# MLA scores of a hybrid attention layer: 289 contracted rows as 128 + 128 + 33 instead of 97 + 96 + 96

## The chip, the cores and the metric

The kernel runs on one core of a Trainium2 chip (trn2). The metric is device time in microseconds (us), the median of three runs; lower is better. The engines of the core are TensorE (PE, its weight loads listed apart as PEld), VectorE (DVE), ScalarE (ACT), GpSimd (POOL) and SyncE (SP, which here issues DMAs).

## The reference, cut to what matters

One layer in float32. From one input projection it computes two token mixers over the same 2048 latent tokens and 256 context tokens, gates them, projects them and merges them. The mixer that the change touches is multi-head latent attention (MLA, 8 heads):

```python
qa = concatenate([qa_n, rope_2d(qa_r)], -1)        # 64 + 32 = 96 columns a head
ka = concatenate([ka_n, broadcast(rope_2d(kr))])   # 64 of the head, 32 shared by all heads
sc = einsum('bqhd,bkhd->bhqk', qblk, k) * 96 ** -0.5
p  = softmax(sc, axis=-1)                          # over 2048 latent and 256 context keys
o  = einsum('bhqk,bkhd->bqhd', p, v)
```

The other mixer is a neighbourhood attention over a 32 x 64 grid; its matmuls are woven into the same stretch of the kernel.

## The kernel before, in words

Float32 accuracy comes from splitting a factor into a high and a low part (type float32r) and adding three products: high x high, high x low, low x high. A first part of the kernel (projections, to about 1057 us) writes the split queries `qm` and keys `kmS`, `krS` to DRAM; a last part (from about 2185 us) does the output projections. The change lies in the attention between them.

That attention goes over `u` = 0 to 31, a head `h` and a block `g` of 512 queries each. For each `u` there are nine steps `kp` (L1262), and each step handles two key tiles `x` of 128 keys. For one key tile the score tile `S` (128 keys x 512 queries, one PSUM bank) is the sum of three matmuls (L1275): `Kh` (96 rows of the high keys and a row of ones) with `qh` (96 rows of the high queries and a row with minus the maximum of each query), 97 contracted rows; `Kh` with `ql` (low queries), 96; `Kl` (low keys) with `qh`, 96. ScalarE then writes `P` = exp(`S`) (L1278).

Around the scores the order of TensorE is the order of the program (L809 pins it). `more` (L1264) issues tasks of the next `u`: 20 matmuls `pm` with the keys, whose maxima VectorE takes (L824, L825), and a fold. In a step of the middle of a `u` two of them stand behind the first score tile and one at the end of the step. `row` (L831), in step 8, turns the maxima into the row of `qh` by a matmul `pmf` and a ScalarE copy (L834). `feed` (L1171) issues the items of the neighbourhood attention (`ns` scores, `nm` and `nc` maxima, `nf`), by a weight, twice a step: behind the first score tile (L1283) and at the end (L1304). `pv` (L1229) multiplies `P` with the values; it collects two steps, so that steps 2, 4, 6 and 8 hold a burst of eight matmuls `oacc`, step 0 one of four, and steps 1, 3, 5 and 7 none. `oacc` is in float32 with 64 columns of weights, the even key tile in one half of the array's columns and the odd one in the other. `zp` and `nz` use quarters of 32 columns. `held` keeps the neighbourhood's own products `no` (also 64 columns) for the end of a burst (L1296).

All of `S`, `pm`, `pmf`, `zp`, `ns`, `nm`, `nc`, `nf` take their PSUM bank from one rotation of five (`psm`, L140): three turns in a pool of three banks and two in a pool of two; a tile waits until the last reader of the bank that it gets is done. GpSimd adds up `P` for the denominators (`za`, L1288) and spreads the maxima (L812). Queries are loaded by `load_qh` and `load_ql` (L773, L779), keys by `load_k` and `load_rope` (L785, L795), on SP's queue; the first of them are issued early, in the first part of the kernel. `P` has 8 buffers (`PB`), the spread maxima `nmd` of the neighbourhood two (L904).

Of the kernel before, what the change touches and what calls it, by code (L numbers as in the profile page):

```python
# [19 lines left out]
P = 128  # L20
# [7 lines left out]
NOPE = 64  # L28
# [26 lines left out]
STAT0 = 300  # L55
NQ = 8
HELD = 2
PB = 8
ZDVE = {1: tuple(range(1, 9))}
NPB = 6  # L60
BIG = -float(2 ** 100)
# [3 lines left out]
def tile_hybrid_layer(ctx: ExitStack, tc: tile.TileContext, I: dict, out: bass.AP, dbg=None):  # L65
# [43 lines left out]
    def bc(ap):  # L109
        return ap.bitcast(F32)  # L110
# [656 lines left out]
    KA = na.tile([P, NK], F32R, name="KA")  # L767
    KBt = na.tile([113, NK], F32R, name="KBt")
    QQ = na.tile([P, S], F32R, name="QQ")
    Kh = [(mk0, mk)[i].tile([DK + 1, NK], F32R, name=f"Kh{i}") for i in range(2)]  # L770
    Kl = [(mk0, mk)[i].tile([DK, NK], F32R, name=f"Kl{i}") for i in range(2)]

    def load_qh(u):  # L773
        h, g = divmod(u, NB)
        qh = mq.tile([DK + 1, W], F32R, tag="qh", name=f"qh{u}", bufs=3)
        env["q"].dma_start(bc(qh[0:DK, :]), bc(qm[h][0, :, g * W:(g + 1) * W]))
        return qh

    def load_ql(u):  # L779
        h, g = divmod(u, NB)  # L780
        ql = mq.tile([DK, W], F32R, tag="ql", name=f"ql{u}")
        env["q"].dma_start(bc(ql), bc(qm[h][1, :, g * W:(g + 1) * W]))
        return ql

    def load_k(h):  # L785
        i = h % 2
        env["q"].dma_start(bc(Kh[i][0:NOPE, :]), bc(kmS[h][0]))
        env["q"].dma_start(bc(Kl[i][0:NOPE, :]), bc(kmS[h][1]))

    def load_v(h):  # L790
        vt = mv.tile([P, NKT, DV], F32, tag="V", name=f"V{h}")
# [1 line left out]
        return vt  # L793

    def load_rope(i):  # L795
        env["q"].dma_start(bc(Kh[i][NOPE:DK, :]), bc(krS[:, 0, :]))
        env["q"].dma_start(bc(Kl[i][NOPE:DK, :]), bc(krS[:, 1, :]))
        nc.gpsimd.memset(bc(Kh[i][DK:DK + 1, :]), 1.0)

    zdefer = []  # L800
    onesr = mz.tile([P, P], F32R, name="onesr", bufs=1)
# [4 lines left out]
    def mm(*args, **kw):  # L806
        ins = nc.tensor.matmul(*args, **kw)  # L807
        if pe["pin"]:
            tc.keep_in_program_order(ins)  # L809
# [2 lines left out]
        nc.gpsimd.tensor_tensor(dst, ident.unsqueeze(1).to_broadcast([P, 4, P]), col.unsqueeze(2).to_broadcast([P, 4, P]),  # L812
                                op=ALU.mult)

    def max_tasks(u, qh):
        i = (u // NB) % 2
        m5 = mq.tile([P, 4, 5], F32, tag="m5", name=f"m5{u}")
        m1 = mq.tile([P, 4], F32, tag="m1", name=f"m1{u}")
        md = mq.tile([P, 4, P], F32R, tag="md", name=f"md{u}", bufs=1)

        def part(qt, ci):
            a, b = ci * W, min(NK, (ci + 1) * W)
            pm = psm(f"pm{u}_{qt}_{ci}")
            mm(pm[:, :b - a], qh[0:DK, qt * P:(qt + 1) * P], Kh[i][0:DK, a:b], start=True, stop=True)  # L824
            nc.vector.reduce_max(m5[:, qt, ci:ci + 1], pm[:, :b - a], axis=AX.X)  # L825

        def fold():
            nc.vector.tensor_reduce(m1, m5, axis=AX.X, op=ALU.max, negate=True)
            spread(md, m1)

        def row():  # L831
            pm = psm(f"pmf{u}")
            mm(pm, onesr, md.rearrange("p t f -> p (t f)"), start=True, stop=True)
            nc.scalar.activation(qh[DK:DK + 1, :], pm[DK:DK + 1, :], AF.Copy)  # L834
            for f in zdefer:
                f()
            zdefer.clear()

        return [lambda q=qt, c=ci: part(q, c) for qt in range(4) for ci in range(5)] + [fold], row
# [31 lines left out]
    def n_max(h, bn):  # L871
        mx = nv.tile([P, 2, 16], F32, tag="nmx", name=f"nmx{h}")
        m1 = nv.tile([P, 16], F32, tag="nm1", name=f"nm1{h}")
        kg = grid(NKm[:, 0:S])
        neg = -3.0e38

        def win(qb):
            rb, cb = divmod(qb, 4)
            (r0, r1), (c0, c1) = NROW[rb], CREG[cb]
            nr, ncl = r1 - r0, c1 - c0  # L880
            pm = psm(f"nm{h}_{qb}")
            pv_ = pm[:, :nr * ncl].rearrange("p (r c) -> p r c", c=ncl)
            mm(pv_, NQs[:, qb * P:(qb + 1) * P], kg[:, r0:r1, c0:c1], start=True, stop=True)
            rr, cc_ = r0 - rb * 8 + 4, c0 - cb * 16 + 8
            jk = npl.tile([P, W], F32, tag="njk", name=f"njk{h}_{qb}", bufs=1)
            nc.vector.tensor_tensor_reduce(
                out=jk[:, :nr * ncl].rearrange("p (r c) -> p r c", c=ncl), in0=pv_,
                in1=bn[:, rr:rr + nr, cc_:cc_ + ncl], scale=1.0, scalar=neg,
                op0=ALU.add, op1=ALU.max, accum_out=mx[:, 0, qb:qb + 1])

        def cmax(b2):
            pm = psm(f"nc{h}_{b2}")
            for x in range(2):
                qb = 2 * b2 + x
                mm(pm[:, x * C:(x + 1) * C], NQs[:, qb * P:(qb + 1) * P], NKm[:, S:NK],
                                 start=True, stop=True)
            nc.vector.reduce_max(mx[:, 1, 2 * b2:2 * b2 + 2], pm.rearrange("p (x c) -> p x c", x=2), axis=AX.X)

        mds = [None] * 4

        def turn(rb):
            if rb == 0:
                nc.vector.tensor_reduce(m1, mx.rearrange("p t q -> p q t"), axis=AX.X, op=ALU.max, negate=True)
            mds[rb] = npl.tile([P, 4, P], F32R, tag="nmd", name=f"nmd{h}_{rb}")  # L904
            spread(mds[rb], m1[:, rb * 4:rb * 4 + 4])

        def fin(rb):
            pm = psm(f"nf{h}_{rb}")
            mm(pm, onesr, mds[rb].rearrange("p t f -> p (t f)"), start=True, stop=True)
            nc.vector.tensor_copy(rowcol(QLt[64:65, rb * W:(rb + 1) * W]), blk(pm[64:65, :]))  # L910

        o = []
        for b2 in range(8):
            o += [lambda q=2 * b2: win(q), lambda q=2 * b2 + 1: win(q), lambda b=b2: cmax(b)]

        def last(k):
            if k < 4:
                turn(k)
            if k > 0:
                fin(k - 1)  # L920

        return o + [lambda k=k: last(k) for k in range(5)]

# [219 lines left out]

    with tc.high_priority(offset=HOIST):
        env["q"] = nc.sync
        qhs = [load_qh(0)]
        load_rope(0)
        load_k(0)
        qls = [load_ql(0)]
        qhs.append(load_qh(1))  # L1150
        env["q"] = nc.sync
    nc.sync.dma_start(bc(NKm[64:NM, :]), bc(cS[0][0:48, :]))
    nc.sync.dma_start(bc(NQs[64:NM, :]), bc(cS[1][0:48, 0:S]))
# [6 lines left out]
    load_rope(1)  # L1160
    env["q"] = nc.sync
    with tc.high_priority(offset=HOIST):
        tasks, row = max_tasks(0, qhs[0])
        for f in tasks + [row]:
            f()

# [79 lines left out]
    for u in range(nu):  # L1246
        h, g = divmod(u, NB)
        i = h % 2
        qh, ql = qhs[u], qls[u]
        vt = Vt  # L1250
        tasks, row = [], None
        if u + 2 < nu:
            qhs.append(load_qh(u + 2))
        if u + 1 < nu:
            tasks, row = max_tasks(u + 1, qhs[u + 1])
        if g == NB - 1 and h + 1 < H:
            Vt = load_v(h + 1)
        acc = psO.tile([P, W], F32, tag="O", name=f"oacc{u}")
# [3 lines left out]
        for kp in range(NKP):  # L1262
            pt = mp.tile([P, 2, W], F32, tag="P", name=f"P{u}_{kp}", bufs=PB)
            def more(frac):  # L1264
                nonlocal done
                want = min(len(tasks), int(len(tasks) * (kp + frac) / (NKP - 2.0) + 1))
                while done < want:
                    tasks[done]()
                    done += 1

            for x in range(2):
                ks = slice((2 * kp + x) * P, (2 * kp + x + 1) * P)
                sp = psm(f"S{u}_{kp}_{x}")
                n = 0
                for a, b, e in ((Kh[i], qh, DK + 1), (Kh[i], ql, DK), (Kl[i], qh, DK)):  # L1275
                    mm(sp, a[0:e, ks], b[0:e, :], start=(n == 0), stop=(n == 2))
                    n += 1
                nc.scalar.activation(pt[:, x, :], sp, AF.Exp)  # L1278
                more(0.33 * x)
                if x == 0 and kp == NKP - 1 and row is not None:  # L1280
                    row()
                if x == 0:
                    feed(total_weight * (step + 0.5 - LEAD) / (nsteps - TAIL - LEAD))  # L1283
            ve = nc.vector if kp in ZDVE.get(nu - u, ()) else nc.gpsimd
            if kp == 1:
                ve.tensor_tensor(za, prev, pt, op=ALU.add)
            elif 1 < kp < NKP - (u + 1 == nu):
                ve.tensor_tensor(za, za, pt, op=ALU.add)  # L1288
            prev = pt
            if kp == 1 and u + 1 < nu:  # L1290
                qls.append(load_ql(u + 1))
            if g == 0 and kp == 1 and h + 1 < H:
                load_k(h + 1)
            if pend is not None:
                ftasks = pv(*pend) or ftasks
                if env.pop("burst", False):  # L1296
                    while held:
# [246 lines left out]
```

## Time and profile before

| what | value |
|---|---|
| median of 3 runs | 2565.34 us (2562.31 to 2571.34) |
| the profiled execution: time | 2569.03 us |
| the profiled execution: span | 2567.2 us |
| mean granted TensorE clock | 0.987 |
| PE busy, all of the span | 2505.7 us (98%) |
| PE busy, 1057 to 2185 us | 1097.56 of 1128 us |

A busy time is a union of instructions of an engine, and a matmul's own duration contains the way through the array, so that durations of neighbours overlap. What a matmul costs in a stream is read from the distance of two starts. `128*64` in a row is the part of the array that is used, rows by columns. A releaser behind `<-` is what ended an engine's idle time.

### The profile page before, as it was taken

The numbers are of one execution on the slowest core, as the hardware profiler recorded it, in microseconds if no ns is written. First come the engines' busy times: TensorE is split into PE (matmuls) and PEld (weight loads), VectorE is DVE, ScalarE is ACT, GpSimd is POOL, SyncE is SP. The second block draws the span as 40 slices with busy tenths as digits, with TensorE's granted clock in tenths as the row PEclk, the third lists the DMA queues.
The fourth block names the chain that finished last, engine by engine and source line by source line (L and its number), as shares of the span: only waits on it lengthen the run. The fifth ranks groups of instructions, "written<-read, shape, count | busy, mean of one in ns | idle before, by whom it ended". The sixth has DMA issues, their size and how long they took to land.

```text
span 2567.2 us, 34839 instructions
## 1 busy us (share of the span) xinstructions
PE 2505.7 (98%) x12796; PEld 1839.1 (72%) x12796; DVE 1102.7 (43%) x2285; ACT 905.3 (35%) x1774; POOL 1092.2 (43%) x861
## 2 busy tenths in 40 slices
PE   7999999999999999999999999999999999999998
PEld 4878888877789888656555656665656664888998
DVE  4653222222311211355455635554646446455654
ACT  3664432222222122234444434444444444212221
POOL 1312111111310000368787868777887885132220
PEclk9999999999999999999999989999999999999999
DMA  7535765456553465712324141514140334765542
GB/s 263 191 92 164 257 222 185 140 167 191 178 159 109 122 214 194 184 48 68 80 51 107 46 101 36 121 39 109 39 110 26 81 106 144 246 190 161 181 148 70
DMA packets 182979, 342.86 MB, mean 134 GB/s; under 512 B 25130, under 2 KB 95950, under 8 KB 175438
## 3 DMA queue, kind: packets, MB, share of 16 engines
q1 hardware_dynamic: 168872, 299.01, 38.9%
q0 software_dynamic: 13504, 41.35, 5.6%
q8 instruction: 100, 1.64, 0.3%
q14 instruction: 71, 0.58, 0.1%
q10 hardware_dynamic: 432, 0.28, 0.0%
HBM read 214.42 MB, written 126.13 MB: 133 GB/s over the span
## 4 chain that ended last, share of the span: by engine, by line
PE 88%; DVE 3%; DMA 3%; POOL 2%; issue 2%; ACT 1%; SPq 1%; POOLq 0%; ACTq 0%; DVEq 0%
PE accm L135 25%; PE S L807 15%; PE oacc L807 10%; PE pm L807 6%; PE f L135 5%; PE ya L135 4%; PE vacc L135 4%; PE nacc L226 3%; PE no L807 3%; PE accf L135 2%; PE accx L135 1%; PE qa_False L135 1%; PE pstl L185 1%; PE nm L807 1%; POOL za L1288 1%
## 5 line engine op out<-in xcount | busy, mean ns | idle before, releaser
L825 DVE TENSOR_REDUCE m<-pm 128x1 f32<-128x512 f32 (+1 forms) x640 | 387.6, 632 | 420.0 <-PE pm L807 414.3
L1288 POOL TENSOR_TENSOR za<-za,P 128x1024 f32<-128x1024 f32 x217 | 516.1, 2378 | 114.2 <-ACT P L1278 110.7
L1278 ACT ACTIVATE P<-S 128x512 f32<-128x512 f32 x576 | 342.9, 597 | 481.3 <-PE S L807 465.9
L135 PE MATMUL accm<-hh,whi 128*128 128x512 f32 x928 | 366.7, 395 | 0.0
L135 PE MATMUL accm<-hh,wlo 128*128 128x512 f32 x928 | 366.4, 395 | 0.0
L135 PE MATMUL accm<-hl,whi 128*128 128x512 f32 x928 | 366.3, 395 | 0.0
L807 PE MATMUL oacc<-P,V 128*64 128x512 f32 x1152 | 292.0, 624 | 0.0
L807 PE MATMUL S<-qh,Kh 97*128 97x512 f32 x576 | 240.4, 417 | 7.9 <-DVE m L825 4.3
L807 PE MATMUL S<-ql,Kh 96*128 96x512 f32 x576 | 230.7, 400 | 0.0
L807 PE MATMUL S<-qh,Kl 96*128 96x512 f32 x576 | 229.3, 398 | 0.0
L807 PE MATMUL pm<-Kh,qh 96*128 96x512 f32 (+1 forms) x640 | 222.6, 395 | 4.5 <-DVE m L825 3.3
L135 PEld LDWEIGHTS accm<-hh,whi 128*128 128x128 f32 x928 | 174.1, 188 | 42.8 <-issue 0.8
L135 PEld LDWEIGHTS accm<-hh,wlo 128*128 128x128 f32 x928 | 174.1, 188 | 42.5
L135 PEld LDWEIGHTS accm<-hl,whi 128*128 128x128 f32 x928 | 174.1, 188 | 41.6
L807 PEld LDWEIGHTS pm<-Kh,qh 96*128 96x128 f32 x640 | 121.1, 189 | 106.7 <-issue 62.5
L135 PE MATMUL ya<-u,woh 128*128 128x256 f32 x1024 | 185.0, 283 | 2.0 <-DVE t L1346 2.0
L807 PEld LDWEIGHTS oacc<-P,V 128*64 128x64 f32 x1152 | 70.4, 139 | 137.6 <-issue 137.3
L135 PE MATMUL f<-wfh,y 128*128 128x512 f32 (+1 forms) x528 | 162.2, 387 | 6.2 <-DMA wfh<-wfS 4.0
L135 PEld LDWEIGHTS ya<-u,woh 128*128 128x128 f32 x1024 | 160.1, 192 | 3.2 <-DVE t L1346 2.4
L807 PEld LDWEIGHTS S<-qh,Kh 97*128 97x128 f32 x576 | 109.9, 191 | 54.0 <-issue 12.4
L135 PE MATMUL ya<-u,wol 128*128 128x256 f32 x512 | 144.8, 283 | 0.0
L356 ACT ACTIVATE g<-accm 128x512 f32<-128x512 f32 x88 | 52.2, 593 | 248.8 <-PE accm L135 202.6
(1928 smaller groups left out, 4253.2 us busy)
## 6 DMA issues: line engine op xcount, KB each, us to landing
rawc<-in_wch SPq DMA_DIRECT2D x30, 512.0 KB
KA<-kB SPq DMA_DIRECT2D x16, 576.0 KB
xl<-in_xb SPq DMA_DIRECT2D x32, 256.0 KB
wm<-in_wmodb SPq DMA_DIRECT2D x8, 1024.0 KB
kmS<-sk POOLq DMA_DIRECT2D x32, 256.0 KB, 3.8
qR<-q SPq DMA_DIRECT2D x16, 512.0 KB
qm<-sq POOLq DMA_DIRECT2D x32, 256.0 KB, 4.1
woS<-ps SPq DMA_DIRECT2D x16, 512.0 KB
```

Of the source, the lines that this page charges most:

```text
L135: nc.tensor.matmul(acc, a, b, start=(i == 0), stop=(i == n - 1))
L185: nc.tensor.matmul(pst[32 * j:32 * j + 32, :w], ones[:, 0:32], sq[:, :w], start=(kt < 4), stop=(kt >= 4))
L226: nc.tensor.matmul(acc[:, :n], a[:, k, sl], b[:, k, :n], start=(k == 0 and q == 0), stop=(k == KT - 1 and q == 2))
L356: nc.scalar.activation(s1, acc, AF.Sigmoid)
L807: ins = nc.tensor.matmul(*args, **kw)
L825: nc.vector.reduce_max(m5[:, qt, ci:ci + 1], pm[:, :b - a], axis=AX.X)
L1278: nc.scalar.activation(pt[:, x, :], sp, AF.Exp)
L1288: ve.tensor_tensor(za, za, pt, op=ALU.add)
```

## The change

The three products of a score tile have 97 + 96 + 96 = 289 contracted rows in all. They are laid out anew as 128 + 128 + 33. `Ka` and `Kb` hold the 96 rows of the high keys, and below them 32 rows each of the low keys of the head; `qa` holds the 96 high rows of the queries and, against the low keys, high rows 0 to 31 again; `qb` the 96 low rows and high rows 32 to 63. What is left are the 32 low rows of the shared rotary key and the row of ones: `Kc` and `qc`, 33 rows. `Kc` has them twice, for even key tiles from partition 0 and for odd ones from partition 64, and the two matmuls of a step with 33 rows stand next to each other, in rows 0 to 63 and 64 to 127 of the array, one for each key tile.

A step therefore issues: `Ka`, `Kb` of the first tile, tasks, `Ka`, `Kb` of the second, tasks, then both matmuls of 33 rows, then both exponentials, and only then the first `feed`, which stood between the tiles. The row of maxima is written twice, to `qc`. Loads: six a `u` for the queries in place of two, four a head for the keys in place of two. `PB` goes from 8 to 7, `nmd` from two buffers to one, and in `last` the matmul of one group of maxima now stands ahead of the spread of the next.

```diff
-PB = 8
+PB = 7
...
+    Ka = [(mk0, mk)[i].tile([P, NK], F32R, name=f"Ka{i}") for i in range(2)]
+    Kb = [(mk0, mk)[i].tile([P, NK], F32R, name=f"Kb{i}") for i in range(2)]
+    Kc = mk0.tile([DK + 1, NK // 2], F32R, name="Kc")
+
+    def load_qa(u):
...
+        env["q"].dma_start(bc(qa[0:DK, :]), bc(qm[h][0, :, cs]))
+        env["q"].dma_start(bc(qa[DK:P, :]), bc(qm[h][0, 0:32, cs]))
+        return qa
+
+    def load_qb(u):
...
+        env["q"].dma_start(bc(qb[0:DK, :]), bc(qm[h][1, :, cs]))
+        env["q"].dma_start(bc(qb[DK:P, :]), bc(qm[h][0, 32:NOPE, cs]))
+        for x in range(2):
+            env["q"].dma_start(bc(qc[64 * x:64 * x + ROPE, :]), bc(qm[h][0, NOPE:DK, cs]))
+        return qb, qc
 
     def load_k(h):
         i = h % 2
-        env["q"].dma_start(bc(Kh[i][0:NOPE, :]), bc(kmS[h][0]))
-        env["q"].dma_start(bc(Kl[i][0:NOPE, :]), bc(kmS[h][1]))
+        for t, a in ((Ka[i], 0), (Kb[i], 32)):
+            env["q"].dma_start(bc(t[0:NOPE, :]), bc(kmS[h][0]))
+            env["q"].dma_start(bc(t[DK:P, :]), bc(kmS[h][1, a:a + 32, :]))
...
+    def load_rope_low():
+        kl = krS[:, 1, :].rearrange("p (t x f) -> p t x f", x=2, f=P)
+        for x in range(2):
+            env["q"].dma_start(bc(Kc[64 * x:64 * x + ROPE, :].rearrange("p (t f) -> p t f", f=P)), bc(kl[:, :, x, :]))
+            nc.gpsimd.memset(bc(Kc[64 * x + ROPE:64 * x + ROPE + 1, :]), 1.0)
...
-            nc.scalar.activation(qh[DK:DK + 1, :], pm[DK:DK + 1, :], AF.Copy)
+            for r in (ROPE, DK):
+                nc.scalar.activation(qbs[u][1][r:r + 1, :], pm[r:r + 1, :], AF.Copy)
...
-            mds[rb] = npl.tile([P, 4, P], F32R, tag="nmd", name=f"nmd{h}_{rb}")
+            mds[rb] = npl.tile([P, 4, P], F32R, tag="nmd", name=f"nmd{h}_{rb}", bufs=1)
...
         def last(k):
+            if k > 0:
+                fin(k - 1)
             if k < 4:
                 turn(k)
-            if k > 0:
-                fin(k - 1)
...
+            sps = []
             for x in range(2):
                 ks = slice((2 * kp + x) * P, (2 * kp + x + 1) * P)
                 sp = psm(f"S{u}_{kp}_{x}")
-                n = 0
-                for a, b, e in ((Kh[i], qh, DK + 1), (Kh[i], ql, DK), (Kl[i], qh, DK)):
-                    mm(sp, a[0:e, ks], b[0:e, :], start=(n == 0), stop=(n == 2))
-                    n += 1
-                nc.scalar.activation(pt[:, x, :], sp, AF.Exp)
+                sps.append(sp)
+                mm(sp, Ka[i][:, ks], qa, start=True, stop=False)
+                mm(sp, Kb[i][:, ks], qb, start=False, stop=False)
                 more(0.33 * x)
                 if x == 0 and kp == NKP - 1 and row is not None:
                     row()
-                if x == 0:
-                    feed(total_weight * (step + 0.5 - LEAD) / (nsteps - TAIL - LEAD))
+            for x in range(2):
+                r = slice(64 * x, 64 * x + ROPE + 1)
+                mm(sps[x], Kc[r, kp * P:(kp + 1) * P], qc[r, :], start=False, stop=True)
+            for x in range(2):
+                nc.scalar.activation(pt[:, x, :], sps[x], AF.Exp)
+            feed(total_weight * (step + 0.5 - LEAD) / (nsteps - TAIL - LEAD))
```

## Rows read from the trace of the kernel before

**Rows 1.** The page, parts 1 and 4: busy time, chain that ended last.

```profile
PE 2505.7 (98%) x12796; PEld 1839.1 (72%) x12796; DVE 1102.7 (43%) x2285; ACT 905.3 (35%) x1774; POOL 1092.2 (43%) x861
...
PE 88%; DVE 3%; DMA 3%; POOL 2%; issue 2%; ACT 1%; SPq 1%; POOLq 0%; ACTq 0%; DVEq 0%
PE accm L135 25%; PE S L807 15%; PE oacc L807 10%; PE pm L807 6%; PE f L135 5%; PE ya L135 4%; PE vacc L135 4%; PE nacc L226 3%; PE no L807 3%; PE accf L135 2%; PE accx L135 1%; PE qa_False L135 1%; PE pstl L185 1%; PE nm L807 1%; POOL za L1288 1%
```

**Rows 2.** Attention stretch: length, busy PE PEld DVE ACT POOL, clock, DMA share, GB/s.

```profile
1057.00:2185.00 1128.00, 1097.56 (x5276) 666.45 (x5277) 603.77 (x1207) 494.60 (x890) 860.89 (x513) 0.98 0.32 82
```

**Rows 3.** Groups, forms apart, first matmul of a score: busy, mean ns, idle before.

```profile
L807 PE MATMUL S<-qh,Kh 97*128 97x512 f32 x576 | 240.4, 417 | 7.9 <-DVE m L825 4.3 <-ACT qh L834 0.7 <-ACT np_('c', 0, 1)_12350 L935 0.7
```

**Rows 4.** Timeline of TensorE, a step with a burst: start, us, engine, line, tiles.

```profile
1360.21 0.62 PE L807 MATMUL pm<-Kh,qh 96*128 96x512 f32 x2
1360.67 0.40 PE L807 MATMUL S<-qh,Kh 97*128 97x512 f32 x1
1360.90 0.40 PE L807 MATMUL S<-ql,Kh 96*128 96x512 f32 x1
1361.14 0.39 PE L807 MATMUL S<-qh,Kl 96*128 96x512 f32 x1
1361.46 1.94 PE L807 MATMUL oacc<-P,V 128*64 128x512 f32 x8
1363.33 0.50 PE L807 MATMUL pm<-Kh,qh 96*128 96x512 f32 x1
1363.67 0.40 PE L807 MATMUL S<-qh,Kh 97*128 97x512 f32 x1
```

**Rows 5.** Timeline of TensorE, end of another burst: column halves of two pairs.

```profile
1664.72 0.59 PE L807 MATMUL no<-np_('c', 0, 0)_13371,nv 128*64 128x512 f32 x1
1664.72 0.59 PE L807 MATMUL no<-np_('c', 2, 0)_13425,nv 128*64 128x512 f32 x1
1665.15 0.59 PE L807 MATMUL no<-np_('c', 0, 0)_13371,nv 128*64 128x512 f32 x1
```

**Rows 6.** Timeline, a score tile that waits for a bank read by an exponential.

```profile
1438.64 0.40 PE L807 MATMUL S<-qh,Kl 96*128 96x512 f32 x1
...
1439.13 0.60 ACT L1278 ACTIVATE P<-S 128x512 f32<-128x512 f32 x1 [0.72 <-PE S L807]
...
1439.78 0.50 PE L807 MATMUL S<-qh,Kh 97*128 97x512 f32 x1 [0.16 <-ACT P L1278]
1440.12 0.40 PE L807 MATMUL S<-ql,Kh 96*128 96x512 f32 x1
```

**Rows 7.** One line's instructions, the row of maxima: min/median/max ns, first and last.

```profile
L834 ACT ACTIVATE qh<-pmf x32: 590/591/593, 1057.2 to 2158.5; 1x512 fp32r<-1x512 f32 x32
```

**Rows 8.** Timeline of TensorE, the first score tile of the attention.

```profile
1057.81 0.50 PE L807 MATMUL S<-qh,Kh 97*128 97x512 f32 x1 [0.70 <-ACT qh L834]
```

**Rows 9.** DMA issues by line (count, KB each); one line's issue in ns.

```profile
qh<-qm SPq DMA_DIRECT2D x32, 192.0 KB
...
Kh<-kmS SPq DMA_DIRECT2D x8, 576.0 KB
...
L776 SPq DMA_DIRECT2D qh<-qm x32: 304/374/617, 715.0 to 2097.6; - x32
```

**Rows 10.** One tile's instructions: the spread of maxima on GpSimd.

```profile
L812 POOL TENSOR_TENSOR nmd<-ident,nm x32: 1035/1041/1057, 1110.7 to 2016.7; 128x512 fp32r<-128x512 f32 x32
```

**Rows 11.** Timeline of TensorE in the first part: transposes, one with 32 columns.

```profile
147.54 0.36 PE L226 MATMUL nacc<-nat_hi,hl 128*128 128x416 f32 x1
147.74 0.49 PE L277 MATMUL pt<-ident,nb 128*128 128x128 f32 x3
148.06 0.27 PE L278 MATMUL pt<-ident,nb 128*32 128x128 f32 x1
148.09 0.43 PE L226 MATMUL nacc<-nat_hi,hh 128*128 128x416 f32 x1
148.36 0.35 PE L226 MATMUL nacc<-nat_lo,hh 128*128 128x416 f32 x1
```

More of the change, by code (lines that the diff above doesn't have):

```diff
@@ L769, in tile_hybrid_layer @@
     QQ = na.tile([P, S], F32R, name="QQ")
-    Kh = [(mk0, mk)[i].tile([DK + 1, NK], F32R, name=f"Kh{i}") for i in range(2)]
-    Kl = [(mk0, mk)[i].tile([DK, NK], F32R, name=f"Kl{i}") for i in range(2)]
-    def load_qh(u):
+    Ka = [(mk0, mk)[i].tile([P, NK], F32R, name=f"Ka{i}") for i in range(2)]
+    Kb = [(mk0, mk)[i].tile([P, NK], F32R, name=f"Kb{i}") for i in range(2)]
+    Kc = mk0.tile([DK + 1, NK // 2], F32R, name="Kc")
+    def load_qa(u):
         h, g = divmod(u, NB)
[L775 to L779, printed above, removed]
-        h, g = divmod(u, NB)
-        ql = mq.tile([DK, W], F32R, tag="ql", name=f"ql{u}")
-        env["q"].dma_start(bc(ql), bc(qm[h][1, :, g * W:(g + 1) * W]))
-        return ql
+        cs = slice(g * W, (g + 1) * W)
+        qa = mq.tile([P, W], F32R, tag="qa", name=f"qa{u}", bufs=3)
+        env["q"].dma_start(bc(qa[0:DK, :]), bc(qm[h][0, :, cs]))
+        env["q"].dma_start(bc(qa[DK:P, :]), bc(qm[h][0, 0:32, cs]))
+        return qa
+    def load_qb(u):
+        h, g = divmod(u, NB)
+        cs = slice(g * W, (g + 1) * W)
+        qb = mq.tile([P, W], F32R, tag="qb", name=f"qb{u}")
+        qc = mq.tile([DK + 1, W], F32R, tag="qc", name=f"qc{u}")
+        env["q"].dma_start(bc(qb[0:DK, :]), bc(qm[h][1, :, cs]))
[3 more added lines that the diff above has]
+        return qb, qc
     def load_k(h):
         i = h % 2
-        env["q"].dma_start(bc(Kh[i][0:NOPE, :]), bc(kmS[h][0]))
-        env["q"].dma_start(bc(Kl[i][0:NOPE, :]), bc(kmS[h][1]))
+        for t, a in ((Ka[i], 0), (Kb[i], 32)):
+            env["q"].dma_start(bc(t[0:NOPE, :]), bc(kmS[h][0]))
+            env["q"].dma_start(bc(t[DK:P, :]), bc(kmS[h][1, a:a + 32, :]))
     def load_v(h):
@@ L795, in load_rope @@
     def load_rope(i):
-        env["q"].dma_start(bc(Kh[i][NOPE:DK, :]), bc(krS[:, 0, :]))
-        env["q"].dma_start(bc(Kl[i][NOPE:DK, :]), bc(krS[:, 1, :]))
-        nc.gpsimd.memset(bc(Kh[i][DK:DK + 1, :]), 1.0)
+        for t in (Ka[i], Kb[i]):
+            env["q"].dma_start(bc(t[NOPE:DK, :]), bc(krS[:, 0, :]))
+    def load_rope_low():
[3 more added lines that the diff above has]
+            nc.gpsimd.memset(bc(Kc[64 * x + ROPE:64 * x + ROPE + 1, :]), 1.0)
     zdefer = []
@@ L813, in spread, with max_tasks @@
                                 op=ALU.mult)
-    def max_tasks(u, qh):
+    def max_tasks(u, qa):
         i = (u // NB) % 2
@@ L823, in part @@
             pm = psm(f"pm{u}_{qt}_{ci}")
-            mm(pm[:, :b - a], qh[0:DK, qt * P:(qt + 1) * P], Kh[i][0:DK, a:b], start=True, stop=True)
+            mm(pm[:, :b - a], qa[0:DK, qt * P:(qt + 1) * P], Ka[i][0:DK, a:b], start=True, stop=True)
             nc.vector.reduce_max(m5[:, qt, ci:ci + 1], pm[:, :b - a], axis=AX.X)
@@ L1145, in tile_hybrid_layer @@
         env["q"] = nc.sync
-        qhs = [load_qh(0)]
+        qas = [load_qa(0)]
         load_rope(0)
         load_k(0)
-        qls = [load_ql(0)]
-        qhs.append(load_qh(1))
+        qbs = [load_qb(0)]
+        load_rope_low()
+        qas.append(load_qa(1))
         env["q"] = nc.sync
@@ L1162, in tile_hybrid_layer @@
     with tc.high_priority(offset=HOIST):
-        tasks, row = max_tasks(0, qhs[0])
+        tasks, row = max_tasks(0, qas[0])
         for f in tasks + [row]:
@@ L1248, in tile_hybrid_layer @@
         i = h % 2
-        qh, ql = qhs[u], qls[u]
+        qa, (qb, qc) = qas[u], qbs[u]
         vt = Vt
@@ L1252, in tile_hybrid_layer @@
         if u + 2 < nu:
-            qhs.append(load_qh(u + 2))
+            qas.append(load_qa(u + 2))
         if u + 1 < nu:
-            tasks, row = max_tasks(u + 1, qhs[u + 1])
+            tasks, row = max_tasks(u + 1, qas[u + 1])
         if g == NB - 1 and h + 1 < H:
@@ L1290, in tile_hybrid_layer @@
             if kp == 1 and u + 1 < nu:
-                qls.append(load_ql(u + 1))
+                qbs.append(load_qb(u + 1))
             if g == 0 and kp == 1 and h + 1 < H:
```

## The prediction

> **What bounds the kernel now.** I read the page first: PE is busy 98% of the span, and of the chain that ended last 88% lies on it, 15% in the scores `S`, 10% in `oacc`, 6% in `pm` [rows 1]. No wait stands out, so a change counts by what it adds to or takes from TensorE's stream. Next the stretches: in the attention, 1057 to 2185 us, PE is busy 1097.56 of 1128 us, while POOL, the next, is busy 860.89 and DVE 603.77; the DMA engines are at 0.32 [rows 2]. Then the groups: the first matmul of a score, 576 of them, waited 7.9 us in all [rows 3]. Last the timeline, where the prices of TensorE are the distances of starts [rows 4 to 6].
>
> A matmul of 512 columns costs 0.23 us in the stream: 1360.67, 1360.90, 1361.14 [rows 4]. It costs that with 97 rows or 96; a row less saves nothing, only a matmul less does.
>
> Two matmuls in column halves start together and the next pair 0.43 us later [rows 5], so halves run side by side. But the burst has a price: from the last `S` (1361.14) to the `S` behind the next `pm` (1363.67) pass 2.53 us, and the work in it is 0.23 + 4 x 0.43 + 0.23 = 2.18. The 0.35 that remain are: `oacc` starts 0.32 behind an `S` of 0.23, so 0.09; the eight last 1.87 to `pm` in place of 1.72, so 0.15, which holds the unhidden load of their own first weights (0.05) and 0.10 for leaving; and `pm` to `S` is 0.34 in place of 0.23, so 0.11 [rows 4]. I read this as 0.09 to 0.10 for each change of the array's division, plus the weight load that it leaves uncovered: 0.05 for 64 columns, 0.11 for 128. The same 0.11 stands behind a wait: 1439.78 to 1440.12 is 0.34 [rows 6]. Entering full width thus costs 0.20.
>
> **The change part by part.**
>
> *Matmuls.* Per step, six slots of 0.23 become four and a pair. Side by side the pair takes one slot: 288 steps x (6 - 5) x 0.234 = 67.4 us saved [rows 4]. No row shows halves of rows. The bounds: as column halves, one slot for two [rows 5]; or one after the other, nothing saved. I take the first, the nearest row.
>
> *Switches.* The pair stands alone: ahead of it `Kb` of the second tile at full height, behind it nearly always a full matmul. Entering: a division plus an uncovered load of 128 columns, 0.09 + 0.11 = 0.20, times 288 = 57.6 us. Leaving: 0.20 too, except where the burst follows at once and would have paid its own entry anyway. That needs an empty first `feed`: in the trace 60 of the 160 bursts lie in steps that have no neighbourhood matmul between their two score tiles, as the one of [rows 4]. So 228 exits x 0.20 = 45.6 us. Together 103 us. Bounds for one switch: 0 (rival A) and 0.31, if the pair's two loads of 128 columns follow each other (0.09 + 2 x 0.11); in column halves the two loads cost 0.05 together, that of one, so I stay at 0.20. Nothing hides this: TensorE is the bound.
>
> The Trainium skill, page "TensorEngine Tiling (Array Packing)", section "Key Properties", says that a change of the tiling mode, not of the tile alone, drains TensorE, and it lists halves of rows as a mode like halves of columns. The column halves here agree, with 0.35 us a burst; for halves of rows no run here shows it. By that rule the sum is the one above; without it, rival A's.
>
> *Banks.* The first score tile now ends with the pair, behind the second tile, so its bank is held longer. Count from the start of the pair: the exponential starts 0.49 behind a last matmul and lasts 0.60, and a bank is handed on 0.05 later [rows 6]: free at 1.14. TensorE leaves the pair at 0.43, the item of `feed` takes 0.2 to 0.5, so the fifth tile behind the first score is wanted at about 0.75. Where a burst lies between (1.87, [rows 4]) nothing waits. In steps 1, 3 and 5 of each `u`, 96 in all, the fifth tile is `pm` or the item behind it, and if it gets that bank it waits 0.4 and pays 0.11 for its load: 0.5. Of the five phases of the rotation of three and two banks it must take that bank in two; in two others the sixth tile does, some 0.1 late; else a bank whose maxima VectorE has taken is free. 96 x (0.4 x 0.5 + 0.4 x 0.1) = 23 us; bounds 0 and 48. I take 20.
>
> *The row of maxima.* ScalarE now copies it twice, 0.59 us each, 32 times [rows 7], ahead of both exponentials of step 8. Behind them stands a burst, and ScalarE is busy 494.60 of 1128 us [rows 2]: hidden; with the burst gone it would cost up to 0.6 x 32 = 19 us. The row is needed one score later than before, by the third matmul: the first score of the attention waited 0.70 for it [rows 8], which goes; late next is the bank of VectorE's maxima. -0.7 us.
>
> *Loads.* Queries: six DMAs a `u` for two, 128 + 128 + 64 rows for 192; keys four a head for two, 192 rows for 128 [rows 9]. That is 32 x 256 KB and 8 x 576 KB, 13 MB more; at 82 GB/s and a DMA share of 0.32 [rows 2] they fit. On SP they add 4 x 32 + 2 x 8 issues at 0.37 us [rows 9], 53 us of a queue of its own; stores of results stand behind them and wait 1 to 2 us, unnoticed. The first loads lie in the first part, with time ahead of 1057 us. Cost 0, bounds 0 and 5 us.
>
> *Buffers.* `P` with 7: a `P` is read for about three steps, 7 steps are enough; 0. `nmd` with one: a spread (1.04 us, 32 of them, [rows 10]) can start only when the matmul of the group before is done; on POOL the sums `za` queue behind it, on TensorE `nf`. I put 1 us, bounds 0 and 32 x 1.04 = 33.
>
> **Sum.** -67.4 + 57.6 + 45.6 + 20 - 0.7 + 1 = +56 us. On the profiled execution (2569.03, its span 2567.2 and 1.8 around it) that is 2625; the median shown is 3.7 us lower, so on it 2565.3 + 56 = 2621 us.
>
> **The rivals.**
>
> *A. A half of rows needs no switch (faster).* The place is the entry and exit of the pair. For it speaks that one change of shape is free in this trace: the transpose with 32 columns starts 0.11 behind the third of its like, as they do among themselves (0.49 for three), and the next two `nacc` at 0.03 and 0.30, together the 0.11 of the transpose and 0.19 of a `nacc` [rows 11]. Against it: every product in halves or quarters pays, and the transposes may be run at full width whatever their shape. Then the sum is -67.4 + 20 = -47, 2518 us. It decides by the price of one switch: 516 switches must cost less than 47 / 516 = 0.09 us each, the whole uncovered load away.
>
> The Trainium skill, "TensorE: Matmul & The Clock Gate", section "Measured speedup vs the span model", gives a pack as the time of one matmul plus about 4 ns for each further tile, with no price of entry. By that rule the pair is as in rival A; no run here shows it.
>
> *B. The two halves do not run side by side.* No row has halves of rows, and both read 512 columns at once. Then the 67.4 are not saved: +56 + 67 = +123, 2688 us. Against it: column halves do overlap [rows 5].
>
> *C. The bank waits in all 96 steps and `nmd` blocks POOL.* For it: waits for banks exist already [rows 6]. +56 + 28 + 10 = +94, 2659 us. Against it: the rotation.
>
> *D. Half the price*, loads of the pair covered by the matmul ahead: 516 x 0.10 = 52 in place of 103: +5, no change, 2570 us.
>
> **How the numbers follow.** The forecast 0.60, A 0.17, B 0.10, C 0.07, D 0.06. The likeliest one's own range is 2595 to 2650. Cases of both signs together: low 2530 (most of A left out), high 2685 (B half out). A measurement here tells 0.3%, 7.7 us, from no change. Faster: A and a little of D, 0.19. Same: most of D and the lower edge of the forecast, 0.07. Slower: 0.74.
>
> **What would show it.** Of the profile after: the two matmuls of 33 rows with starts some ns apart (else B); `Kb` to the pair 0.32 or more in place of 0.23, and 0.33 from the pair to the next full matmul, with another 0.11 behind that (else A or D); exponentials in twos; waits of PE for the exponentials' banks of some 20 us, in steps without a burst. The forecast is wrong if the attention gets shorter than 1128 us, or longer by over 100.

## The result and the profile after

| kernel | median, us | range | the kernel before on the same chip | ratio, 95% interval |
|---|---|---|---|---|
| after | 2653.5 | 2645.3 to 2658.3, 4 runs | 2564.6 | 1.0334 [1.0317, 1.0351] |

The change costs 88.9 us; the forecast was 56, 2621 us, with 2530 to 2685 as its range. The time lies inside that range, but above the 2595 to 2650 that the prediction gave for its likeliest case. Sign and mechanism came as argued; a term that the sum had at nothing is worth some 35 us.

The page after, parts 1 and 4, answers to [rows 1]:

```profile
PE 2555.9 (96%) x12796; PEld 1772.6 (67%) x12796; DVE 1106.5 (42%) x2285; ACT 901.1 (34%) x1806; POOL 1093.0 (41%) x861
...
PE 75%; issue 14%; POOL 3%; DMA 3%; DVE 2%; ACT 2%; SPq 0%; POOLq 0%; ACTq 0%; DVEq 0%
```

TensorE still does the same number of matmuls and is busy 50 us longer. The 14% of `issue` are mostly one stretch of the chain, 731 to 1050 us, ahead of the late loads told of below; in run 1, which brings these loads forward, it is 2% again. The stretches say where (columns as in [rows 2]): the seam between the first part and the attention, then the attention.

```profile
1050.00:1085.00 35.00, 11.39 (x23) 5.81 (x21) 11.54 (x22) 0.60 (x1) 4.71 (x6) 0.54 1.03 225
1085.00:2273.00 1188.00, 1143.94 (x5274) 600.19 (x5276) 603.60 (x1207) 489.26 (x919) 856.51 (x508) 0.98 0.33 84
```

The attention grew from 1128 us to 1188. The 35 us ahead of it were not there: the kernel before went from its last `accm` at 1056.07 to its first score at 1057.81 [rows 8]. From first to last score it is 1126.1 before and 1186.9 after, +60.8; up to the first score +27.7; behind the last -4.2. The three make the +84.3 of the two spans.

The seam, TensorE's timeline (start, duration, line, tiles, in brackets the idle time before it and what ended it):

```profile
1049.92 0.40 PE L135 MATMUL accm<-hh,wlo 128*128 128x512 f32 x1
1071.54 11.05 PE L821 MATMUL pm<-Ka,qa 96*128 96x512 f32 x20 [21.22 <-DMA Ka<-kmS]
1084.92 0.80 PE L821 MATMUL pmf<-md,onesr 128*128 128x512 f32 x1 [2.34 <-DMA KBt<-kB]
1085.52 0.63 PE L821 MATMUL S<-qa,Ka 128*128 128x512 f32 x1
1085.94 0.63 PE L821 MATMUL S<-qb,Kb 128*128 128x512 f32 x1
```

In the kernel before, the 20 `pm` of the first queries ran from 863 us on, woven into the first part:

```profile
863.47 0.86 PE L807 MATMUL pm<-Kh,qh 96*128 96x512 f32 x3
...
1056.07 0.39 PE L135 MATMUL accm<-hh,wlo 128*128 128x512 f32 x1
```

Now they stand behind it, after 21 us of idling for the first keys. SP's queue shows why the keys are late: the first load of queries, issued at 715.0 before [rows 9], goes out at 1046.23, and the keys behind it.

```profile
1046.23 0.33 SPq L778 DMA_DIRECT2D qa<-qm x1
...
1056.96 0.93 SPq L796 DMA_DIRECT2D Ka<-kmS x1
```

In the attention, a step that answers to [rows 4]:

```profile
1657.80 0.39 PE L821 MATMUL S<-qa,Ka 128*128 128x512 f32 x1
1658.03 0.39 PE L821 MATMUL S<-qb,Kb 128*128 128x512 f32 x1
1658.35 0.50 PE L821 MATMUL S<-qc,Kc 33*128 33x512 f32 x2
1658.78 0.49 PE L821 MATMUL ns_('w', 1, 2)_13191<-QQ,KA 128*128 128x480 f32 x1
1659.10 0.39 PE L821 MATMUL ns_('w', 1, 2)_13191<-QLt,KBt 113*128 113x480 f32 x1
```

Read the distances of starts. `qa` to `qb` is 0.23, a plain slot. `qb` to the pair is 0.32: 0.09 to go in. The pair (x2 in one row; by the two starts 3 to 4 ns apart) to the next is 0.43: a slot, 0.09 and 0.10. The next, of 480 columns and worth 0.22, takes 0.32: another 0.10. A stay in row halves, from the matmul ahead of it to the second one behind it, thus costs its slot and 0.39. Over 288 stays the median is 0.326 in and 0.429 out. In 58 of them a burst of column halves follows at once, and there the last 0.10 is missing.

The weight loads (PEld) of the same step:

```profile
1657.80 0.19 PEld L821 LDWEIGHTS S<-qb,Kb 128*128 128x128 f32 x1
1658.35 0.19 PEld L821 LDWEIGHTS S<-qc,Kc 33*128 33x128 f32 x2 [0.36 <-issue]
1658.78 0.19 PEld L821 LDWEIGHTS ns_('w', 1, 2)_13191<-QQ,KA 128*128 128x128 f32 x1 [0.24 <-DVE m L839]
1658.88 0.19 PEld L821 LDWEIGHTS ns_('w', 1, 2)_13191<-QLt,KBt 113*128 113x128 f32 x1
```

In a plain stream a load stands a whole slot ahead of its matmul (`Kb`: 1657.80 for 1658.03). Around the stay it does not: the loads of the pair and of the next matmul are shown at the start of these matmuls themselves, and the load behind them 0.10 later.

The groups, with idle time behind the second bar; the first answers to [rows 3]:

```profile
L821 PE MATMUL S<-qa,Ka 128*128 128x512 f32 x576 | 243.1, 422 | 9.0 <-ACT P L1301 4.3 <-DVE m L839 2.9 <-DVE nmx L901 1.2
L821 PE MATMUL pm<-Ka,qa 96*128 96x512 f32 (+1 forms) x640 | 236.1, 420 | 30.2 <-DMA Ka<-kmS 21.2 <-ACT P L1301 6.0 <-DVE m L839 1.6
L821 PE MATMUL nf<-nmd,onesr 128*128 128x512 f32 x32 | 15.5, 485 | 11.8 <-POOL nmd L826 11.4 <-ACT P L1301 0.3
```

Waits for banks that an exponential reads (`ACT P`) are new, some 18 us over all tiles against 2; `nf` for `nmd` was 2.8 before.

### The profile page after: what moved, and what is told of

It reads as the page before. It is cut to its first block, busy times and chain, and to the rows that moved or that the text cites. A ratio compares the mean times of both kernels' runs of the same rounds, so it can differ in the third digit from the quotient of the medians.

```text
span 2651.6 us, 35160 instructions
## 1 busy us (share of the span) xinstructions
PE 2555.9 (96%) x12796; PEld 1772.6 (67%) x12796; DVE 1106.5 (42%) x2285; ACT 901.1 (34%) x1806; POOL 1093.0 (41%) x861
## 4 chain that ended last, share of the span: by engine, by line
PE 75%; issue 14%; POOL 3%; DMA 3%; DVE 2%; ACT 2%; SPq 0%; POOLq 0%; ACTq 0%; DVEq 0%
PE accm L135 16%; PE S L821 15%; PE oacc L821 10%; PE f L135 6%; PE pm L821 6%; PE ya L135 5%; PE nacc L226 3%; PE no L821 3%; ACT P L1301 2%; PE accf L135 2%; PE accx L135 1%; POOL za L1307 1%; PE nm L821 1%; PE qa_False L135 1%; PE pstl L185 1%
## 5 line engine op out<-in xcount | busy, mean ns | idle before, releaser
L1301 ACT ACTIVATE P<-S 128x512 f32<-128x512 f32 x576 | 312.9, 595 | 493.1 <-PE S L821 477.8
L821 PE MATMUL pm<-Ka,qa 96*128 96x512 f32 (+1 forms) x640 | 236.1, 420 | 30.2 <-DMA Ka<-kmS 21.2
L821 PE MATMUL S<-qa,Ka 128*128 128x512 f32 x576 | 243.1, 422 | 9.0 <-ACT P L1301 4.3
L821 PE MATMUL S<-qb,Kb 128*128 128x512 f32 x576 | 229.8, 399 | 0.0
L821 PEld LDWEIGHTS pm<-Ka,qa 96*128 96x128 f32 x640 | 123.3, 194 | 153.4 <-issue 87.9
L821 PEld LDWEIGHTS S<-qa,Ka 128*128 128x128 f32 x576 | 109.8, 191 | 58.7 <-issue 15.2
L821 PE MATMUL S<-qc,Kc 33*128 33x512 f32 x576 | 145.8, 503 | 0.0
```

The lines of the kernel that those rows point to most:

```text
L1301: nc.scalar.activation(pt[:, x, :], sps[x], AF.Exp)
```

## The experiments

Excess is the median less that of the kernel before on the same chip (2564.6 to 2568.8), so that chips drop out. Its 95% interval is some 4 to 7 us either way, so a few us between two runs say little.

| run | what | median | excess | ratio, 95% interval |
|---|---|---|---|---|
| | after | 2653.5 | +88.9 | 1.0334 [1.0317, 1.0351] |
| 1 | after, pools moved | 2621.4 | +53.6 | 1.0201 [1.0182, 1.0219] |
| 2 | before, queries' pool pushed up | 2572.9 | +5.1 | 1.0020 [1.0006, 1.0034] |
| 3 | 1 without switches | 2587.4 | +19.7 | 1.0066 [1.0047, 1.0085] |
| 4 | 1 with the pair twice | 2677.1 | +109.3 | 1.0423 [1.0400, 1.0447] |
| 5 | 3 in the old order | 2571.3 | +3.5 | 1.0010 [0.9995, 1.0026] |
| 6 | before, one `nmd` | 2572.2 | +4.4 | 1.0017 [1.0004, 1.0031] |
| 7 | 1 with lone halves | 2751.5 | +183.7 | 1.0710 [1.0690, 1.0730] |
| 8 | 1 with two pairs a stay | 2787.6 | +219.7 | 1.0849 [1.0821, 1.0877] |
| 9 | 8, `pmf` late, two `nmd` | 2665.7 | +100.4 | 1.0386 [1.0361, 1.0412] |
| 10 | after, only keys early | 2633.8 | +65.0 | 1.0253 [1.0238, 1.0269] |
| 11 | after, only queries early | 2651.4 | +82.6 | 1.0316 [1.0295, 1.0337] |
| 12 | 1 with two `nmd` | 2618.4 | +49.6 | 1.0191 [1.0176, 1.0206] |

### Where the first tiles lie: runs 1, 2, 10, 11

The addresses of the two built programs (bytes in a partition of SBUF) differ. With seven buffers of `P` instead of eight, the pool above it moves down 4 KB: the first keys from 64032 to 59936, and the pool `st`, which stands to the end of the first part, reaches up to 61984. The new tiles `Kc` and `qc` push the other end up: the pool of queries ends at 99616 instead of 95008, and `hT3`, in use to the last `accm`, begins at 98272. Run 1 mends both, but for the small pool of `qc`, which still crosses 98272 and is loaded at 1056.16:

```
     mp = pool(m2, "mp", 3)
+    mz = pool(m2, "mz", 2)
     mk0 = pool(m2, "mk0")
     mq = pool(m2, "mq", 2)
+    mqc = pool(m2, "mqc", 2)
...
-    mz = pool(m2, "mz", 2)
...
-        qc = mq.tile([DK + 1, W], F32R, tag="qc", name=f"qc{u}")
+        qc = mqc.tile([DK + 1, W], F32R, tag="qc", name=f"qc{u}")
```

> The changed kernel with its SBUF pools in another order (mz ahead of mk0, the tiles qc in a pool of their own behind mq), so that Ka0, Kb0, Kc, the first qa and qb and the tiles of the row of maxima lie where nothing of the first part stands to its end; instructions are the same. Theory (the 27.7 us by which the first score comes later are a matter of where the tiles lie: the first loads waited for the first part to end, and the 20 pm of the first queries moved out of it): first pm at about 863 us, first score at about 1058 instead of 1085.5, the time 24 to 28 us below the changed kernel, about 2627. Rival (the loads are late because there are more of them, on SP's queue and the DMA engines): first score stays near 1085, the time near 2653.

Its timeline of TensorE:

```profile
863.13 0.86 PE L822 MATMUL pm<-Ka,qa 96*128 96x512 f32 x3
...
1055.96 0.39 PE L822 MATMUL pmf<-md,onesr 128*128 128x512 f32 x1
1056.19 0.39 PE L822 MATMUL S<-qa,Ka 128*128 128x512 f32 x1
```

The `pm` are back at 863 and the first score at 1056. The excess falls by 35.3 us, to 53.6, more than the 24 to 28 expected; the two profiled spans are 31.0 us apart. The loads are as many as in the changed kernel, so the rival falls.

Run 2 puts 4 KB of padding into the kernel before:

```
+    pad = pool(m2, "pad")
+    padt = pad.tile([P, W * 2], F32, name="padt")
     mq = pool(m2, "mq", 2)
```

> The kernel before with 4 KB of padding below the pool of queries, so that this pool reaches into the region of hT3; its loads and matmuls are the same in number. Theory (place of the tiles): the queries are loaded only at the end of the first part, the 20 pm run behind it, first score 12 to 25 us later than 1057.8 (the keys are loaded early here, so less than the 27.7 of the changed kernel), time 2577 to 2590. Rival (number of loads): no difference, 2564.6.

```profile
1042.76 0.33 SPq L778 DMA_DIRECT2D qh<-qm x1
...
1046.45 0.40 PE L135 MATMUL accm<-hh,wlo 128*128 128x512 f32 x1
1049.80 0.93 PE L809 MATMUL pm<-Kh,qh 96*128 96x512 f32 x3 [2.95 <-issue]
...
1064.36 0.79 PE L809 MATMUL S<-qh,Kh 97*128 97x512 f32 x1 [0.68 <-ACT qh L836]
```

The `pm` moved behind the first part as expected, but this cost 5.1 us, not 12 to 25: I had not set off that the first part ends 10 us sooner without them. Of the pool of queries only `md` crosses 98272 here, and yet the queries below it were issued at 1042.76 in place of 715.0: where one tile crosses, the loads of its whole pool come late in these builds.

Run 10 takes the edit of `mz` alone (keys early, queries late); run 11 is run 1 without it (queries early, keys late). Run 11 against run 1:

```
     mp = pool(m2, "mp", 3)
-    mz = pool(m2, "mz", 2)
     mk0 = pool(m2, "mk0")
     mq = pool(m2, "mq", 2)
     mqc = pool(m2, "mqc", 2)
...
+    mz = pool(m2, "mz", 2)
```

> The changed kernel with mz ahead of mk0 alone: Ka0, Kb0 and Kc lie clear of the tiles of the first part that stand to its end, the pool of queries still reaches into that of hT3. Theory (what TensorE waited 21.2 us for were the keys, issued on SP behind the queries and both behind the end of the first part): with the keys in early it is as the second run showed for the kernel before, pm behind the end of the first part with only a short wait, first score at about 1066, 5 to 10 us above the first run, 2627 to 2632. Rival (either late load costs all): near the changed kernel, 2653.

> The first run with mz back behind mk: the queries and the tiles of the row of maxima lie clear of the first part's last tiles, the keys of the first head do not. Theory as in the run before: the keys come late, TensorE waits for them behind the first part; their issue no longer stands behind eight issues of queries (1046 instead of 1057), so the first pm comes at about 1062 and the first score at about 1075: 15 to 22 us above the first run, 2636 to 2643. Rival (the queries were the wait): near the first run, 2621.

Run 10, then run 11:

```profile
1054.11 1.07 PE L821 MATMUL pm<-Ka,qa 96*128 96x512 f32 x3 [3.56 <-DMA qa<-qm]
...
1067.81 0.63 PE L821 MATMUL S<-qa,Ka 128*128 128x512 f32 x1
```

```profile
1065.63 11.05 PE L822 MATMUL pm<-Ka,qa 96*128 96x512 f32 x20 [16.30 <-DMA Ka<-kmS]
...
1079.61 0.63 PE L822 MATMUL S<-qa,Ka 128*128 128x512 f32 x1
```

Over run 1, late queries alone cost 11.4 us (5 to 10 were expected), late keys alone 29.0, both 35.3. It is mostly the keys that TensorE waits for. For run 11 I expected 15 to 22; the first score came at 1079.6, not 1075. The DMA engines were full there (share 0.95 in 1046 to 1080); that this is the reason is not shown.

### The switch: runs 3, 4, 7

```
-                r = slice(64 * x, 64 * x + ROPE + 1)
-                mm(sps[x], Kc[r, kp * P:(kp + 1) * P], qc[r, :], start=False, stop=True)
+                mm(sps[x], Kc[:, kp * P:(kp + 1) * P], qc, start=False, stop=True)
```

> The kernel of the first run with the third matmul of each score tile at full height (97 rows) in the same place, so six slots a step and no change of the array's division for it; the low parts of both tiles of a step are summed into each. Theory (switches cost more than the slot that they save: 0.20 in and 0.20 out by the prediction, 0.39 by the distances in the trace of the changed kernel): 288 x 0.234 = 67 us of matmuls come back and 103 to 112 of switches go, so 36 to 45 us below the first run, about 2587. What then remains above the kernel before, 15 to 25 us, is bank waits and the waits of nf. Rival A (rows need no switch): 67 us above the first run, about 2694. Rival C (the loss is bank waits): these stay, the matmuls come back, above the first run by 40 to 67.

```profile
L824 PE MATMUL S<-qc,Kc 97*128 97x512 f32 x576 | 182.0, 397 | 0.2 <-DMA qc<-qm 0.2
```

```profile
1640.50 0.40 PE L824 MATMUL S<-qb,Kb 128*128 128x512 f32 x1
1640.73 0.63 PE L824 MATMUL S<-qc,Kc 97*128 97x512 f32 x2
```

One more slot a step, and 34.0 us less, just under the 36 to 45 expected. With the 67.4 of those slots the switches of run 1 cost 101.4 us; the forecast had 103.2. The starts say the same: run 1 less run 3, above the slots, is 0.39 for each of the 224 stays ahead of a full matmul and 0.20 for each of the 58 right ahead of a burst, with the 6 others 100.5 us in all. Rival A is out by 101 us. Waits for `ACT P` stay in this run (3.7 for `S`, 5.0 for `pm`), so they belong to the order, not to the halves.

Run 4 issues the pair twice:

```
+            for y in range(2):
                 for x in range(2):
...
-                mm(sps[x], Kc[r, kp * P:(kp + 1) * P], qc[r, :], start=False, stop=True)
+                    mm(sps[x], Kc[r, kp * P:(kp + 1) * P], qc[r, :], start=False, stop=(y == 1))
```

> The kernel of the first run with the pair of row halves issued twice, the second pair directly behind the first (the last 33 rows are counted twice, with half the maximum in each). Theory (both halves of a pair run side by side, and the price is paid on entering and leaving, not by the pair): 288 x 0.234 = 67 us above the first run, about 2694. Rival B (halves one after the other): 135 us above, about 2762. Rival D (each pair pays its loads): 67 plus 0.1 to 0.2 a step, 96 to 125 us above.

```profile
1658.45 0.40 PE L822 MATMUL S<-qb,Kb 128*128 128x512 f32 x1
1658.77 0.74 PE L822 MATMUL S<-qc,Kc 33*128 33x512 f32 x4
1659.44 0.39 PE L822 MATMUL pm<-Ka,qa 96*128 96x256 f32 x1
```

Two pairs last 0.67 where one lasts 0.43: 0.24 more, one slot. The whole kernel grew by 55.7 us, under the 67; some 8 us of waits for POOL and for banks went, the rest is not told apart. Rival B would have been 135: the halves run side by side.

Run 7 puts each tile's 33 rows behind its own two matmuls:

```
                 mm(sp, Kb[i][:, ks], qb, start=False, stop=False)
+                r = slice(64 * x, 64 * x + ROPE + 1)
+                mm(sp, Kc[r, kp * P:(kp + 1) * P], qc[r, :], start=False, stop=True)
+                nc.scalar.activation(pt[:, x, :], sp, AF.Exp)
                 more(0.33 * x)
```

> The kernel of the first run with the order of the kernel before: each tile's matmul of 33 rows stands behind its own two full ones, so that a step has two lone row halves in place of one pair. Theory (a stay in row halves costs one slot of 0.234 and 0.29 of going in and out, whether one half works or both; bank waits of 15 us go): 288 x 0.52 = 151 less 15, 136 us above the first run, about 2757. Rival D (a lone half is cheaper, as it loads one set of weights): 288 x (0.234 + 0.18) - 15 = 104 above, about 2725. Rival A (no price): 67 - 15 = 52 above, about 2673.

```profile
1659.17 0.40 PE L822 MATMUL S<-qb,Kb 128*128 128x512 f32 x1
1659.49 0.50 PE L822 MATMUL S<-qc,Kc 33*128 33x512 f32 x1
1659.92 0.62 PE L822 MATMUL pm<-Ka,qa 96*128 96x512 f32 x2
```

0.32 in and 0.43 out, as for a pair: the price is of the stay, and rival D's cheaper lone half falls. The total, 130.1 us over run 1 for 136, is near the expectation partly by luck: its 0.29 left out the 0.10 behind the next matmul, and also that a stay right ahead of a burst costs less. Run 5 below has the same order at full height, so run 7 less run 5 is nearly the price alone: 180.2 us for 576 stays, 0.31 each; by the starts 0.36 ahead of a full matmul (415 stays) and 0.20 ahead of a burst (159).

### The smaller terms: runs 5, 6, 12

Run 5 is run 3 in the old order (the lines behind the two tiles go):

```
                 mm(sp, Kb[i][:, ks], qb, start=False, stop=False)
+                mm(sp, Kc[:, kp * P:(kp + 1) * P], qc, start=False, stop=True)
+                nc.scalar.activation(pt[:, x, :], sp, AF.Exp)
                 more(0.33 * x)
...
+                if x == 0:
+                    feed(total_weight * (step + 0.5 - LEAD) / (nsteps - TAIL - LEAD))
```

> The kernel of the third run (third matmul at full height, the low parts of both tiles of a step summed into each) with the order of the kernel before: third matmul and exponential right behind the first two of each tile, the first feed between the two tiles. Theory (the later end of the first tile costs bank waits, 17 us of waits for P in the trace of the third run, with 0.1 for each restart): 14 to 18 us below the third run, 2569 to 2574, which leaves 2 to 6 us above the kernel before for the waits of nf. Rival (these waits only take the place of others): no change, 2587.

16.2 us below run 3, and of the waits for `ACT P` only 3.0 us are left: the price of the later end of the first tile. The 3.5 us that remain can't be told from no change.

Run 6 has this edit in the kernel before; run 12 takes it back in run 1.

```
-            mds[rb] = npl.tile([P, 4, P], F32R, tag="nmd", name=f"nmd{h}_{rb}")
+            mds[rb] = npl.tile([P, 4, P], F32R, tag="nmd", name=f"nmd{h}_{rb}", bufs=1)
...
+            if k > 0:
+                fin(k - 1)
             if k < 4:
                 turn(k)
-            if k > 0:
-                fin(k - 1)
```

> The kernel before with the one part of the change that is outside the scores: one buffer for nmd, and in the last five tasks of the maxima the matmul of block k-1 ahead of the spread of block k. Theory (each spread now waits for the matmul of the block before, and the next matmul for the spread: nf waits for POOL 11.4 us in place of 2.8): 8 to 10 us above the kernel before, about 2576. Rival (the time would have been waited elsewhere): no change, 2567.

> The first run with two buffers for nmd again and the last five tasks of the maxima in the order of the kernel before. Theory (11.6 us of waits of nf for POOL against 2.8 in the kernel before, and a restart of 0.1 at each): 8 to 10 us below the first run, about 2612. Rival (as in the sixth run, half of it would be waited elsewhere): 4 below, 2617.

```profile
PE nf L807 <- POOL nmd L812: 13.3, 11, 2.8
PE pmf L807 <- POOL md L812: 8.0, 6, 3.0
PE S L807 <- DVE m L825: 4.5, 8, 1.0
```

This is run 6: total, times, longest. In the kernel before they were:

```profile
PE pmf L807 <- POOL md L812: 11.8, 6, 3.0
...
PE nf L807 <- POOL nmd L812: 2.8, 1, 2.8
```

`nf` waits 10.5 us longer than before, `pmf` 3.8 less. The net is 4.4 in run 6, between the theory's 8 to 10 and the rival's nothing, and 4.0 in run 12, the rival's number; run 12's interval overlaps that of run 1, run 6's excludes no change.

### Two pairs in one stay: runs 8, 9

If the price is the stay's, two steps should share one, right ahead of the burst. The tasks of the next `u` and the items of `feed` then come behind the burst, no longer between the score tiles:

```
-        for kp in range(NKP):
+        for kps in [(0, 1), (2, 3), (4, 5), (6, 7), (8,)]:
...
+            for n, kp in enumerate(kps):
+                for x in range(2):
+                    r = slice(64 * x, 64 * x + ROPE + 1)
+                    mm(sps[2 * n + x], Kc[r, kp * P:(kp + 1) * P], qc[r, :], start=False, stop=True)
...
+            for p_ in pends:
+                ftasks = pv(*p_) or ftasks
```

> On the first run: the scores of two steps (four tiles, in four of the five banks) one after the other, then both pairs in one stay in row halves, then the burst of column halves of the two steps before, then the other work of both steps (a held pair of the neighbourhood part is worked off sooner where its buffers would not last). Theory (the price is one of each stay, and the burst's own entry is saved): 67 us of matmuls saved against the kernel before, 160 stays of 0.28 less the burst's 0.09 = 31 us paid, nf 9 us: 27 us below the kernel before, 2541, plus what the waits for banks come to now that four of five are held at once; by 0.1 to 0.4 us for each of 144 double steps that is 14 to 58 us, so 2555 to 2600. Rival (price of each pair): 67 us saved, 288 x 0.29 = 84 paid, nf 9 and the same bank waits: 2608 to 2652.

```profile
PE pmf L822 <- POOL md L827: 67.5, 29, 5.9
PE nf L822 <- POOL nmd L827: 39.0, 18, 4.4
PE pm L822 <- DVE m L840: 9.0, 27, 0.9
```

The kernel is slower by 220 us, both numbers missed: TensorE waits 106.5 us for POOL, which now gets its sums of two steps at once with `md` behind them, and the granted clock of the attention falls to 0.93. Run 9 moves `pmf` to the end of its step and gives `nmd` two buffers (the edit of run 6 taken back):

```
-            if kps[0] == NKP - 1 and row is not None:
-                row()
...
                 step += 1
+            if kp == NKP - 1 and row is not None:
+                row()
```

> The kernel of the eighth run with two repairs: the matmul of the row of maxima (pmf) stands at the end of the last step of each u instead of at its start, and nmd has two buffers again with the old order of the last five tasks. Theory (the eighth run lost its gain to TensorE's waits for POOL, 67.5 us of pmf for md and 39 of nf for nmd, and to the lower granted clock behind them, 0.93 in the attention against 0.98): the waits fall to about 10 to 15 us and the clock goes back to 0.97 or 0.98, 160 to 225 us below the eighth run, 2560 to 2625. Rival (four scores in a row starve TensorE of banks whatever the row does): only the waits themselves go, about 100, 2690.

```profile
PE nf L822 <- POOL nmd L827: 16.2, 8, 4.0
PE pm L822 <- DVE m L840: 11.9, 29, 2.1
PE S L822 <- DVE m L840: 5.4, 10, 1.8
```

119 us come back, between the theory's 160 to 225 and the rival's 100, and the kernel still has an excess of 100. Going in and out did get cheaper: above their slots (0.234 for 512 columns), the starts around row halves add up to some 50 us, in run 1 to some 95. But starts between full matmuls grew by some 97 us (206 against 109 above their slots): waits for the maxima of VectorE and POOL, each with a load of 0.10 behind it, and a clock of 0.96 in the attention where run 1 has 0.99. Waits for banks that an exponential reads are down to 0.2 us. How the 97 divide was not tried apart; whether the cause is that four of five banks are held at once, or that the other work comes in a row behind the burst, is not shown. No kernel here beats the one before.

## Why the prediction was right in sign and 33 us short

| term | forecast | measured | by |
|---|---|---|---|
| slots saved | -67.4 | -67 (two pairs 0.67, one 0.43) | run 4 |
| switches | +103.2 | +101.4 | 1 against 3 |
| bank waits | +20 | +16.2 | 3 against 5 |
| `nmd` | +1 | +4 | 6, 12 |
| row of maxima | -0.7 | not tried apart | |
| first loads | 0 (0 to 5) | +35.3 | after against 1 |

*Switches.* The total stands, its parts were laid out wrong. The forecast had 0.20 on entering, with an uncovered load of 128 columns in it; the entry is 0.09 in all. On leaving it had 0.20, and 0.29 came: 0.09, 0.10 before the next matmul and 0.10 before the one after, which I read as two uncovered loads. Run 4 confirms that the first 0.10 belongs to whatever follows the pair: a second pair takes it, and what follows the second pair starts 0.10 sooner. The 60 exits into a burst that the forecast took off are 58 here, and they do cost 0.19 less.

The Trainium skill, "TensorEngine Tiling (Array Packing)", section "Key Properties", says that a change of the tiling mode drains TensorE. For halves of rows the runs now show a price, 0.39 us a stay; that it is a drain no row shows. The Trainium skill, "TensorE: Matmul & The Clock Gate", section "Measured speedup vs the span model", gives a pack as one matmul and about 4 ns for each further tile. This holds within the pair (3 to 4 ns between the starts); the 0.39 of going in and out comes on top.

*The step that failed* is "The first loads lie in the first part, with time ahead of 1057 us. Cost 0, bounds 0 and 5 us". That time was there because the tiles lay where nothing stood to the end of the first part. The change moved them, by the constant of `P` and the new tiles `Kc` and `qc`, all in the diff, but the term weighed volume and queue, not addresses; the term for `P`, at 0, asked only how long a `P` is read. The runs put +35.3 us in its place: late keys alone 29.0 (run 11), late queries alone 11.4 (run 10). Without this term the forecast of +56 stands against +53.6 in run 1.

*`nmd`* was put at 1 with bounds to 33; it is 4. *The row*: the first wait of 0.70 was to go; in run 1 TensorE waits 1.02 us for the row, one score tile later. *Rival C*, 2659 us, gave nearly the measured time by the wrong mechanism: bank waits were 16, not 48.

## What to carry to other kernels

A pack of the array is worth its slots less the price of every stay: here 0.234 saved against 0.39 paid, or 0.20 right ahead of a burst that changes the division anyway. So it could pay only there, or where several packs share a stay, and then the order that this takes must not cost more in waits, as it did in runs 8 and 9. When a change adds tiles or alters a buffer count, compare where the pools of the next part lie against what the last part still holds: an overlap of 2 KB cost 29 us. A work order that is denser for one engine hands its bursts to the others; look at who releases it before counting the gain.

## What the runs showed of the hardware

In the seam of after, 1050 to 1085, where TensorE idled for 21 us, the granted clock was 0.54, mostly the lower of its two levels (1.2 GHz): scores started 0.42 apart (1085.52, 1085.94) in place of 0.23. It stayed there while TensorE was already busy again (length, busy PE PEld DVE ACT POOL, clock, DMA share, GB/s):

```profile
1085.00:1090.00 5.00, 5.00 (x11) 2.81 (x12) 0.99 (x2) 3.48 (x5) 0.00 (x0) 0.50 1.01 179
...
1095.00:1100.00 5.00, 5.00 (x12) 2.43 (x14) 1.36 (x3) 1.31 (x3) 2.66 (x2) 0.50 1.02 218
1100.00:1110.00 10.00, 9.58 (x41) 4.86 (x38) 5.71 (x14) 2.17 (x4) 6.08 (x3) 0.97 0.47 108
```

With run 1 the attention took 1183.9 us from first to last score, 3.1 less than after. And a lone half of the array costs as much to enter and leave as a full pair: 0.327 in and 0.427 out by the medians of run 7.
